# The experts gather x over its norm, and scale and shift go in as columns where the gathered rows leave PSUM

## The chip, the cores and the metric

The kernel runs on one core of one Trainium2 chip, in one launch. The metric is the time of the device for one execution, in microseconds (us): lower is better. A core has five engines with a queue of instructions each, which every engine works off in order: TensorE (PE; its weight loads are listed as PEld), VectorE (DVE), ScalarE (ACT), GpSimd (POOL) and SyncE (SP), which here issues the transfers from memory (DMA). Data are worked on in SBUF, which has 128 partitions; matmuls write into PSUM, which DVE and ACT read.

## The reference, cut to what matters

Two transformer blocks in a row on 256 tokens of width 1024, in float32. The first block has two layers, and each layer has a mixer (attention of several kinds) and a mixture of 16 experts. The change touches the mixture of experts alone:

```
sh_m, sc_m, g_m, shift_f, scale_f, gate_f = adaln(c, ada_w[layer], ada_b[layer])
h = rmsnorm(x, norm_ffn[layer]) * (1 + scale_f) + shift_f       # 256 x 1024
# grouped_moe(h, ...):
aff = sigmoid(h @ router_w)                  # 256 x 16 experts, in 4 groups of 4
# one group of experts is picked by aff + router_b, and 2 experts in it (TOP_K)
# each token's row h goes through its experts, weighted by aff over its sum:
#   y_e = (silu(h @ w_gate[e]) * (h @ w_up[e])) @ w_down[e]      # 1024 -> 512 -> 1024
x = x + gate_f * sum_e weight_e * y_e
```

rmsnorm divides each token's row by the root of its mean square (the factor is `rs` in the kernel) and multiplies by a gain per column. Scale, shift and gate depend on one condition vector `c`, so that they are the same for all tokens: one number for each of the 1024 columns. The kernel holds the scale with the gain in it as `mod[4]` and the shift as `mod[3]`, both 128x1024 with the same row in every partition.

## The kernel before

The first block's weights come through a ring of 12 slots of 1 MB each, which SP fills in the order of use: an expert's gate and up weights are two slots each, its down weights two. A slot is free again when the last matmul on it is done. The order of instructions on each engine is set when the program is built, by a scheduler that works with a time line of its own, and is then fixed; each engine's queue runs in that order and waits where an operand is not there.

The token rows are in `s.x[0]` and `s.x[1]`, 128 tokens each. `moe_body` first prepares the router:

- PE transposes x (L187, by way of `trans4`), ACT and DVE copy the transposes out (`hTf`). ACT and DVE sum the squares (L1913, L1914), POOL makes `rs` (L1916).
- The router's weights were multiplied by the scale ahead of time (`router_prep`, L1105 to L1120, which transposes `mod[4]` and `mod[3]` to have scale and shift along the partitions). So the logits are 8 matmuls with the transposed x (L1920), a copy `lg` (L1922), 4 small matmuls (L1925), then `z` with `rs` and the shift's part on DVE (L1927), and the sigmoid `aff` on ACT (L1928), which first loads its table.
- A chain of small DVE operations picks group and experts: `bz` (L1931), `s`, `gs`, `gm`, `gt`, `ge` (L1936 to L1950), `sel` (L1954, L1955), and its bf16 copy `selb` (L1957).
- PE counts the tokens of each expert with three small matmuls on `selb`, DVE makes each token's place `pos` (L1970) and from it the one-hot matrices `OH` (L1976): per expert 64 columns, one for each place.

Beside that chain the rows to be gathered are made: h = x * rs * mod[4] on DVE (L1984), + mod[3] on POOL (L1985), then the high part `hTh` on ACT (L1988) and the rest `hTl` on DVE (L1989). These two read h in steps of 8 elements (32 bytes), so that each block of 128 columns of the result is one k of 8, as the expert weights have it (column p * 8 + k in partition p).

`gather(b)` (L2011 to L2024) then forms the experts' inputs for four experts at a time: 32 matmuls, with 128 columns of `hTh` or `hTl` as weights and 256 columns of `OH` as the moving operand, into 4 banks of PSUM, which ACT copies to `xT`. It is called 4 times per layer. `gateup` (L2048) and `down` (L2066) are the experts' own matmuls, on two experts at a time. Tokens that find no place among the 64 of an expert go through an overflow loop (L2126 to L2232) that gathers them with the same operands (L2212, copy `xk` L2215); it runs once here, in the second layer.

While the router works, PE also has matmuls for the next scale, shift and gate rows (`ada`, L1046 to L1099): 8 matmuls of 512 columns for a row (L1095), `adat` on DVE (L1098), one matmul that spreads it over the partitions (L1057), and a copy `mod` (L1059, L1061).

The code around the change, with the profile's line numbers:

Of the kernel before, what the change touches and what calls it, by code (L numbers as in the profile page):

```python
# [57 lines left out]
class Kern:  # L58
# [125 lines left out]
    def trans4(s, src, n=4):  # L184
        p = s.bank("tp", (128, n, 128))
        for i in range(n):
            s.nc.tensor.transpose(p[:, i], src[:, i * 128:(i + 1) * 128], s.ident)  # L187
        return p

# [650 lines left out]
class Full(Kern):  # L840
# [108 lines left out]
    def setup1(s):  # L949
# [14 lines left out]
        nc.gpsimd.memset(s.rwg, 0.0)  # L964
        s.rlb = B1.tile([128, 16], F32, name="rlb")
        s.onesb = B1.tile([128, 128], BF, name="onesb")
        nc.gpsimd.memset(s.onesb, 1.0)
        s.trib = B1.tile([128, 128], BF, name="trib")
        s.rb = B1.tile([128, 16], F32, name="rb")
        s.late.append(lambda: nc.sync.dma_start(s.rwp, I["router_w"].rearrange("(k p) e -> p k e", p=128)))  # L970
        s.late.append(lambda: nc.sync.dma_start(s.rb, I["router_b"].partition_broadcast(128)))
# [133 lines left out]
    def router_prep(s):  # L1105

        nc, V = s.nc, s.nc.vector
        for j in range(2):
            p = s.trans4(s.mod[4][:, j * 512:(j + 1) * 512])
            V.tensor_tensor(s.rwg[:, 4 * j:4 * j + 4, 0:16], s.rwp[:, 4 * j:4 * j + 4], p[:, :, 0:16], op=OP.mult)  # L1110
            yield
        q = s.bank("bg", (128, 16))
        for j in range(2):
            p = s.trans4(s.mod[3][:, j * 512:(j + 1) * 512])
            sh = s.a2("sh")
            nc.scalar.copy(sh, p)
            for k in range(4):
                nc.tensor.matmul(q, sh[:, k], s.rwp[:, 4 * j + k], start=j + k == 0, stop=j + k == 4)
        V.tensor_copy(s.rlb, q)
        yield  # L1120
# [754 lines left out]
    def moe_srcs(s, l):  # L1875
# [4 lines left out]
        for e in range(0, 16, 2):  # L1880
            for w in (g, u):
                for h in range(2):
                    for i in range(2):
                        out.append((w[e + i].rearrange("(p k) n -> p k n", p=128)[:, 4 * h:4 * h + 4], True))
            for h in range(2):
                for i in range(2):
                    out.append((d[e + i].rearrange("(p k) n -> p k n", p=128)[:, 2 * h:2 * h + 2], True))
# [7 lines left out]
    def moe_body(s, l, end):  # L1895
# [10 lines left out]
        for t in range(2):  # L1906
            for j in range(2):
                p = s.trans4(s.x[t][:, j * 512:(j + 1) * 512])
                if t == 0:
                    nc.scalar.copy(hT[j][:, :, 0:128], p)  # L1910
                else:
                    V.tensor_copy(hT[j][:, :, 128:256], p)
# [8 lines left out]
        lg = s.a2("lg", (128, 256))  # L1921
        nc.scalar.copy(lg, p)  # L1922
        p = s.bank("bg", (128, 2, 16))
        for t in range(2):
# [31 lines left out]
        selb = A.tile([128, 2, 16], BF, name="selb")  # L1956
        V.tensor_copy(selb, sel)  # L1957
        W = f("W", 2, 16)
# [14 lines left out]
        def onehot(b):  # L1973
            for t in range(2):
                e = slice(4 * b, 4 * b + 4)
                V.tensor_tensor(OH[t][:, e], pos[:, t, e, None].to_broadcast([128, 4, 64]), s.C["io1"][:, None, :].to_broadcast([128, 4, 64]),  # L1976
                                op=OP.is_equal)

        hh = []
        for t in range(2):  # L1980
            h = hb[t]
            hi = s.hp.tile([128, D], F32R, name=f"hTh{t}")
            lo = s.hp.tile([128, D], F32R, name=f"hTl{t}")
            V.scalar_tensor_tensor(h, s.x[t], rs[:, t:t + 1], s.mod[4], op0=OP.mult, op1=OP.mult)  # L1984
            G.tensor_tensor(h, h, s.mod[3], op=OP.add)  # L1985

            hv, hiv, lov = h.rearrange("t (p k) -> t k p", k=8), *(x.rearrange("t (k p) -> t k p", k=8) for x in (hi, lo))
            nc.scalar.copy(hiv, hv)  # L1988
            V.tensor_tensor(lov, hv, hiv.bitcast(F32), op=OP.subtract)  # L1989
            hh.append((hi, lo))  # L1990
        OH += [s.sm.tile([128, 16, 64], F32R, name=f"OH{t}", tag="h", bufs=2) for t in range(2)]
# [19 lines left out]
        def gather(b):  # L2011
            for i in range(2):
                xT[2 * b + i] = A.tile([128, 8, 128], F32, name="xT", tag="xT", bufs=3)
            for c in range(0, 8, 2):
                p = s.bg()
                for cc in range(2):
                    first = True
                    for t in range(2):
                        for x in hh[t]:
                            nc.tensor.matmul(p[:, cc * 256:(cc + 1) * 256], x[:, (c + cc) * 128:(c + cc + 1) * 128], OH[t][:, 4 * b:4 * b + 4],  # L2020
                                             start=first, stop=t == 1 and x is hh[t][1])
                            first = False
                for i in range(2):
                    nc.scalar.copy(xT[2 * b + i][:, c:c + 2], p.rearrange("p (c i s) -> p c i s", c=2, i=2)[:, :, i])  # L2024

# [100 lines left out]
    def overflow(s, l, hh, pos, W, nx, cum):  # L2126
# [44 lines left out]
        with s.tc.For_i(0, n, 1):  # L2171
# [9 lines left out]
            for h in range(2):  # L2181
                for i, w in enumerate(("moe_w_gate", "moe_w_up")):
                    nc.sync.dma_start(*s.flat(wg[2 * h + i], I[w][l][e].rearrange("o (p k) n -> p (o k) n", p=128)[:, 4 * h:4 * h + 4]))
            tail()
# [23 lines left out]
            for c in range(8):  # L2208
                first = True
                for t in range(2):  # L2210
                    for x in hh[t]:
                        nc.tensor.matmul(p[:, c], x[:, c * 128:(c + 1) * 128], oh[:, t, 0], start=first, stop=t == 1 and x is hh[t][1])  # L2212
                        first = False
            xk = s.a2("xk", (128, 8, 64))
            nc.scalar.copy(xk, p)  # L2215
            p = s.bank("tp", (128, 2, 128))
# [49 lines left out]
```

## Time and profile before

| | before |
|---|---|
| median of 3 runs | 2464.49 us (2462.65 to 2467.65) |
| profiled execution | 2464.17 us |
| its span in the trace | 2462.4 us |
| mean granted TensorE clock | 0.972 of full speed |
| busy: PE, PEld | 2310.5 us (94%), 1636.8 us (66%) |
| busy: DVE, ACT, POOL | 1297.5 us, 1031.8 us, 411.6 us |

The span is the time from the first to the last event in the trace; 1.8 us of the execution lie around it. A busy share is an average over the program; what a change in one place is worth is read there. TensorE runs at one of two clocks, 1.2 and 2.4 GHz, and the trace tells what share of full speed was granted in a stretch.

### The profile page before, as it was taken

To read this page: it belongs to the slowest core of one execution; us is meant where nothing else is said; L and a number is where in the kernel's file an instruction comes from. 1 tells how busy PE (TensorE), PEld (TensorE's weight loads), DVE (VectorE), ACT (ScalarE), POOL (GpSimd) and SP (SyncE) were. 2 spreads that over 40 slices of the span, in tenths; PEclk is the share of its full clock that TensorE was granted. 3 is DMA by queue.
4 is the path that set the end of the run, shared out by engine and by line. 5 is a ranking of instruction groups with operands and counts; after the bars stand their busy time and mean duration, and the time that the engine had idled before them with its cause. 6 is when DMAs were issued, how large, how long until landed. Compare 5 with 4: busy or idle time off the path is not lost.

```text
span 2462.4 us, 32028 instructions
## 1 busy us (share of the span) xinstructions
PE 2310.5 (94%) x12635; PEld 1636.8 (66%) x12635; DVE 1297.5 (53%) x2047; ACT 1031.8 (42%) x1615; POOL 411.6 (17%) x356
## 2 busy tenths in 40 slices
PE   6999999989899898999888999999999997999999
PEld 4755433356443436888777788887887776788887
DVE  4455222255422226555777756555555877765554
ACT  3454111044211105445655564444444754564543
POOL 1001000010100002002468510000001439620000
PEclk8999999989999898999999999999999998999999
DMA  9677798966799795555333355654655442445552
GB/s 346 242 262 255 320 420 365 415 231 232 290 419 382 300 383 189 188 190 198 132 139 121 138 168 170 204 187 163 205 188 195 167 142 90 135 159 196 172 188 69
DMA packets 241657, 551.33 MB, mean 224 GB/s; under 512 B 12639, under 2 KB 113864, under 8 KB 216160
## 3 DMA queue, kind: packets, MB, share of 16 engines
q1 hardware_dynamic: 241504, 549.26, 61.9%
q8 instruction: 100, 1.64, 0.3%
q14 instruction: 53, 0.43, 0.1%
HBM read 548.15 MB, written 1.06 MB: 223 GB/s over the span
## 4 chain that ended last, share of the span: by engine, by line
PE 62%; DVE 8%; POOL 5%; issue 2%; ACT 2%; DVEq 0%; ACTq 0%; POOLq 0%
PE mm L135 10%; PE mm L137 10%; PE mm L136 10%; PE mm L2048 5%; PE m L135 4%; PE m L136 4%; PE m L137 4%; DVE lo L917 3%; PE m L2066 2%; PE tp L187 2%; PE bg L136 2%; PE bg L135 2%; PE bg L137 2%; POOL rb L597 1%; PE bg L2020 1%
## 5 line engine op out<-in xcount | busy, mean ns | idle before, releaser
L917 DVE TENSOR_TENSOR lo<-w,hi 128x1024 fp32r<-128x1024 f32 (+1 forms) x520 | 659.5, 1308 | 422.0 <-issue 117.7
L915 ACT CAST hi<-w 128x1024 fp32r<-128x1024 f32 (+1 forms) x524 | 519.6, 1040 | 464.5 <-DVE lo L917 352.6
L135 PE MATMUL mm<-hi,hTh 128*128 128x512 f32 (+2 forms) x1200 | 482.4, 404 | 16.4 <-DVE rx L594 8.7
L136 PE MATMUL mm<-lo,hTh 128*128 128x512 f32 (+2 forms) x1200 | 473.4, 395 | 1.0 <-DVE lo L917 1.0
L137 PE MATMUL mm<-hi,hTl 128*128 128x512 f32 (+2 forms) x1200 | 471.9, 394 | 2.1 <-DVE hTl L192 1.8
L135 PEld LDWEIGHTS mm<-hi,hTh 128*128 128x128 f32 x1200 | 228.9, 191 | 65.4 <-DVE rx L594 10.2
L137 PEld LDWEIGHTS mm<-hi,hTl 128*128 128x128 f32 x1200 | 228.8, 191 | 53.3 <-DVE hTl L192 4.2
L2048 PE MATMUL mm<-w,xT 128*64 128x512 f32 x1024 | 259.4, 600 | 2.9 <-DVEq L2171 1.6
L136 PEld LDWEIGHTS mm<-lo,hTh 128*128 128x128 f32 x1200 | 229.7, 192 | 45.1 <-DVE lo L917 1.8
L2048 PEld LDWEIGHTS mm<-w,xT 128*64 128x64 f32 x1024 | 80.8, 137 | 141.4 <-issue 136.5
L135 PE MATMUL m<-hi,hTh 128*128 128x512 f32 x384 | 156.0, 407 | 9.2 <-DVE rx L594 8.9
L137 PE MATMUL m<-hi,hTl 128*128 128x512 f32 x384 | 153.4, 399 | 0.6 <-DVE hTl L192 0.6
L136 PE MATMUL m<-lo,hTh 128*128 128x512 f32 x384 | 153.7, 400 | 0.0
L2066 PE MATMUL m<-w,hidT 128*64 128x512 f32 x512 | 123.7, 597 | 7.7 <-ACT hidT L2059 6.6
L2053 DVE TENSOR_TENSOR sl<-mm,sl 128x512 f32<-128x512 f32 x16 | 11.1, 691 | 160.9 <-PE mm L2048 116.4
L135 PEld LDWEIGHTS m<-hi,hTh 128*128 128x128 f32 x384 | 73.9, 193 | 26.8 <-DVE rx L594 10.2
L2066 PEld LDWEIGHTS m<-w,hidT 128*64 128x64 f32 x512 | 41.1, 136 | 72.8 <-issue 61.5
L2071 DVE SCALAR_TENSOR_TENSOR yf<-m,wsl,mod 128x512 f32<-128x512 f32 x32 | 24.0, 750 | 114.9 <-PE m L2066 113.2
L137 PEld LDWEIGHTS m<-hi,hTl 128*128 128x128 f32 x384 | 73.6, 192 | 16.2 <-DVE hTl L192 1.0
L136 PEld LDWEIGHTS m<-lo,hTh 128*128 128x128 f32 x384 | 73.9, 192 | 15.3 <-DVE lo L917 0.8
L204 POOL TENSOR_TENSOR rs<-ss,mhalf 128x1 f32<-128x1 f32 x18 | 11.0, 611 | 427.1 <-DVE ss L202 427.0
L191 ACT CAST hidh<-tp 128x256 fp32r<-128x256 f32 x88 | 32.3, 372 | 101.2 <-PE tp L187 101.1
(610 smaller groups left out, 3492.5 us busy)
## 6 DMA issues: line engine op xcount, KB each, us to landing
w<-in_ffn_w_in_dram SPq DMA_DIRECT2D x176, 512.0 KB, 4.9
w<-in_w_in_dram SPq DMA_DIRECT2D x84, 1024.0 KB, 4.9
w<-in_moe_w_gate_dram SPq DMA_DIRECT2D x64, 1024.0 KB, 10.8
w<-in_moe_w_up_dram SPq DMA_DIRECT2D x64, 1024.0 KB, 13.9
w<-in_moe_w_down_dram SPq DMA_DIRECT2D x64, 1024.0 KB, 12.3
w<-in_ada_w_dram SPq DMA_DIRECT2D x48, 1024.0 KB, 7.4
w<-in_ffn_w_out_dram SPq DMA_DIRECT2D x44, 1024.0 KB, 4.9
w<-in_ev_w_in_dram SPq DMA_DIRECT2D x10, 1024.0 KB, 6.6
```

Source lines behind the costliest of these rows:

```text
L135: nc.tensor.matmul(out, xh, wh, start=first, stop=False)
L136: nc.tensor.matmul(out, xh, wl, start=False, stop=False)
L137: nc.tensor.matmul(out, xl, wh, start=False, stop=last)
L187: s.nc.tensor.transpose(p[:, i], src[:, i * 128:(i + 1) * 128], s.ident)
L191: s.nc.scalar.copy(hi, p)
L597: G.tensor_tensor(b[:, :, o:o + 64], x[:, :, i:i + 64], sn[:, t, None, o:o + 64].to_broadcast([128, 4, 64]), op=OP.mult)
L915: a = s.nc.scalar.copy(hi[:, h], t[:, h]).ins
L917: b = eng.tensor_tensor(lo[:, h], t[:, h], hi[:, h].bitcast(F32), op=OP.subtract).ins
L2020: nc.tensor.matmul(p[:, cc * 256:(cc + 1) * 256], x[:, (c + cc) * 128:(c + cc + 1) * 128], OH[t][:, 4 * b:4 * b + 4], start=first, stop=t ...
L2048: nc.tensor.matmul(p[64 * i:64 * i + 64], xT[q][:, 4 * h + k, 64 * i:64 * i + 64], ws[i][:, k], start=h + k == 0, stop=h + k == 4)
L2066: nc.tensor.matmul(ps[n][64 * i:64 * i + 64], hT[:, 2 * h + k, 64 * i:64 * i + 64], ws[i][:, k, n * 512:(n + 1) * 512], start=h + k == 0, ...
L2071: V.scalar_tensor_tensor(yf, ps[n], wsl[:, q:q + 1], s.mod[5][:, n * 512:(n + 1) * 512], op0=OP.mult, op1=OP.mult)
```

## The change

What is gathered is no longer h, but x * rs, split in a high and a low part. Scale and shift, which stand along the partitions once the rows are gathered and transposed, are put in as one column each when a bank of gathered rows is read out of PSUM. The columns come from the transposes of `mod[4]` and `mod[3]` that `router_prep` makes anyway, into a new tile `mT` (128x16). The order of columns that the expert weights need now comes from the matmul's weight operand: the transposes and the gather read every 4th element of their rows (16 bytes apart), and the expert's gate and up weights and the router's weights are loaded in two halves of 512 rows, each with 4 rows per partition.

The evacuation of a gather's bank becomes two activations of 128x128 on ACT (scale and bias as columns) and two operations of 128x128 on DVE, instead of two copies of 128x256 on ACT. In the overflow loop `xk` is made by two operations on DVE instead of one copy on ACT.

```diff
+    def transp(s, src, j):
+        p = s.bank("tp", (128, 4, 128))
+        v = src[:, j * 512:(j + 1) * 512].rearrange("t (p k) -> t k p", k=4)
+        for k in range(4):
+            s.nc.tensor.transpose(p[:, k], v[:, k], s.ident)
+        return p
...
-            p = s.trans4(s.mod[4][:, j * 512:(j + 1) * 512])
+            p = s.transp(s.mod[4], j)
+            V.tensor_copy(s.mT[:, 4 * j:4 * j + 4], p[:, :, 0])
...
-            p = s.trans4(s.mod[3][:, j * 512:(j + 1) * 512])
+            p = s.transp(s.mod[3], j)
             sh = s.a2("sh")
             nc.scalar.copy(sh, p)
+            V.tensor_copy(s.mT[:, 8 + 4 * j:12 + 4 * j], sh[:, :, 0])
...
-                        out.append((w[e + i].rearrange("(p k) n -> p k n", p=128)[:, 4 * h:4 * h + 4], True))
+                        out.append((w[e + i, 512 * h:512 * h + 512].rearrange("(p k) n -> p k n", p=128), True))
...
-                p = s.trans4(s.x[t][:, j * 512:(j + 1) * 512])
+                p = s.transp(s.x[t], j)
...
         nc.scalar.copy(lg, p)
+        hh = []
+        for t in range(2):
+            hi = s.hp.tile([128, D], F32R, name=f"hTh{t}")
+            lo = s.hp.tile([128, D], F32R, name=f"hTl{t}")
+            nc.scalar.activation(hi, s.x[t], AF.Copy, scale=rs[:, t:t + 1])
+            hh.append((hi, lo))
+        lows = lambda t: V.scalar_tensor_tensor(hh[t][1], s.x[t], rs[:, t:t + 1], hh[t][0].bitcast(F32), op0=OP.mult, op1=OP.subtract)
+        lows(0)
...
-        V.tensor_copy(selb, sel)
+        q = V.tensor_copy(selb, sel).ins
+        s.after(lows(1).ins, q.name)
+        hh = [[x.rearrange("t (h p k) -> t h k p", h=2, k=4) for x in y] for y in hh]
...
-        hh = []
-        for t in range(2):
-            h = hb[t]
-            hi = s.hp.tile([128, D], F32R, name=f"hTh{t}")
-            lo = s.hp.tile([128, D], F32R, name=f"hTl{t}")
-            V.scalar_tensor_tensor(h, s.x[t], rs[:, t:t + 1], s.mod[4], op0=OP.mult, op1=OP.mult)
-            G.tensor_tensor(h, h, s.mod[3], op=OP.add)
-            hv, hiv, lov = h.rearrange("t (p k) -> t k p", k=8), *(x.rearrange("t (k p) -> t k p", k=8) for x in (hi, lo))
-            nc.scalar.copy(hiv, hv)
-            V.tensor_tensor(lov, hv, hiv.bitcast(F32), op=OP.subtract)
-            hh.append((hi, lo))
...
-                            nc.tensor.matmul(p[:, cc * 256:(cc + 1) * 256], x[:, (c + cc) * 128:(c + cc + 1) * 128], OH[t][:, 4 * b:4 * b + 4],
+                            nc.tensor.matmul(p[:, cc * 256:(cc + 1) * 256], x[:, (c + cc) // 4, (c + cc) % 4], OH[t][:, 4 * b:4 * b + 4],
...
-                for i in range(2):
-                    nc.scalar.copy(xT[2 * b + i][:, c:c + 2], p.rearrange("p (c i s) -> p c i s", c=2, i=2)[:, :, i])
+                for cc in range(2):
+                    m = s.mT[:, c + cc:c + cc + 1], s.mT[:, 8 + c + cc:9 + c + cc]
+                    for i in range(2):
+                        o, x = xT[2 * b + i][:, c + cc], p[:, cc * 256 + i * 128:cc * 256 + i * 128 + 128]
+                        if i:
+                            V.tensor_scalar(o, x, m[0], m[1], op0=OP.mult, op1=OP.add)
+                        else:
+                            nc.scalar.activation(o, x, AF.Identity, bias=m[1], scale=m[0])
...
-                        nc.tensor.matmul(p[:, c], x[:, c * 128:(c + 1) * 128], oh[:, t, 0], start=first, stop=t == 1 and x is hh[t][1])
+                        nc.tensor.matmul(p[:, c], x[:, c // 4, c % 4], oh[:, t, 0], start=first, stop=t == 1 and x is hh[t][1])
...
-            nc.scalar.copy(xk, p)
+            for i, o in enumerate((OP.mult, OP.add)):
+                V.tensor_tensor(xk, xk if i else p, s.mT[:, 8 * i:8 * i + 8, None].to_broadcast([128, 8, 64]), op=o)
```

Left out are the loads of the router's weights and of the overflow loop's expert weights, which are re-laid in the same way. `s.after` pins an instruction behind another in the scheduler's order.

The order of three places follows. A row gives the line in its own kernel, the operation, the tiles written and read, and the shape. First DVE in the second layer's router, from the choice of experts on; before, the two low parts `hTl` and the next row `adat` stand among the choosing operations:

```order
L1950 COPY_PREDICATED gt<-call,ge 128x128
L1940 TENSOR_REDUCE gm<-gs 128x2
L1989 TENSOR_TENSOR hTl_4607<-h,hTh_4606 128x1024
L1954 TENSOR_REDUCE sel<-gt 128x32
L1941 TENSOR_TENSOR gs<-gs,gm 128x8
L1942 TENSOR_TENSOR gs<-gs,call 128x8
L1098 SCALAR_TENSOR_TENSOR adat<-abias,ident,bg 128x512
L1943 TENSOR_REDUCE gm<-gs 128x2
L1989 TENSOR_TENSOR hTl_4613<-h,hTh_4612 128x1024
L1944 TENSOR_TENSOR gs<-gs,gm 128x8
L1955 SCALAR_TENSOR_TENSOR sel<-sel,gs 128x32
L1957 CAST selb<-sel 128x32
```

The same place on DVE in the changed kernel, whose lines from L188 on are numbered higher:

```order
L1961 TENSOR_REDUCE gm<-gs 128x2
L1975 TENSOR_REDUCE sel<-gt 128x32
L1962 TENSOR_TENSOR gs<-gs,gm 128x8
L1963 TENSOR_TENSOR gs<-gs,call 128x8
L1964 TENSOR_REDUCE gm<-gs 128x2
L1965 TENSOR_TENSOR gs<-gs,gm 128x8
L1976 SCALAR_TENSOR_TENSOR sel<-sel,gs 128x32
L1978 CAST selb<-sel 128x32
L1942 SCALAR_TENSOR_TENSOR hTl_4605<-x_71,rs_4559,hTh_4604 128x1024
L1982 TENSOR_TENSOR W<-aff,sel 128x32
L1107 SCALAR_TENSOR_TENSOR adat<-abias,ident,bg 128x512
L1993 SCALAR_TENSOR_TENSOR pos<-tp,sel 128x32
```

Nothing stands any more between the choice and `selb`; one low part and one `adat` stand between `selb` and `pos`. The other low part is further up, behind `z`.

Second, ACT in the second layer's router, before; `lg` is the copy of the logits, `aff` the sigmoid:

```order
L1922 COPY lg<-bg 128x256
L1928 ACT_TABLE_LOAD
L1928 ACTIVATE aff<-z 128x32
L1988 CAST hTh_4606<-h 128x1024
L1061 COPY mod_4622<-bg 128x512
L1988 CAST hTh_4612<-h 128x1024
```

And in the changed kernel:

```order
L1933 COPY lg<-bg 128x256
L1940 ACTIVATE hTh_4601<-x_70,rs_4559 128x1024
L1940 ACTIVATE hTh_4604<-x_71,rs_4559 128x1024
L1949 ACT_TABLE_LOAD
L1949 ACTIVATE aff<-z 128x32
```

Both high parts have moved ahead of the table load and the sigmoid.

Third, DVE in the second layer after the last of the eight one-hot matrices, in the changed kernel, where the first gather's banks are read out (`xT`); before, that work was ACT's alone:

```order
L1999 TENSOR_TENSOR OH_4652<-pos,call 128x256
L1999 TENSOR_TENSOR OH_4653<-pos,call 128x256
L2015 SCALAR_TENSOR_TENSOR nx<-tp,nx 128x16
L1986 TENSOR_TENSOR W<-W,den 128x32
L2038 TENSOR_SCALAR xT<-bg,mT 128x128
L2015 SCALAR_TENSOR_TENSOR nx<-tp,nx 128x16
L2038 TENSOR_SCALAR xT<-bg,mT 128x128
```

The first of DVE's reads of the banks stands behind all eight one-hot matrices, two of which the first gather needs.

## Rows read from the trace of the kernel before

**Rows 1.** Busy time by stretch: us, busy of each engine, PEclk, DMA share, GB/s

```profile
626.00:646.00 20.00, 11.59 (x81) 4.77 (x80) 17.93 (x38) 9.16 (x11) 6.37 (x3) 0.93 1.00 405
253.00:258.00 5.00, 4.84 (x28) 4.42 (x30) 3.24 (x15) 1.48 (x5) 0.00 (x0) 0.53 0.15 34
285.00:312.00 27.00, 27.00 (x138) 11.34 (x135) 6.83 (x11) 4.25 (x10) 0.00 (x0) 1.00 1.01 419
```

**Rows 2.** Chain of waits, 626 to 651 us: start, us, what

```profile
631.59 0.38 ACT lg L1922
...
635.30 1.17 DVE bz L1931
...
636.49 2.54 DVE s L1936 x4
...
639.83 1.91 DVE hTl L1989
...
642.20 0.66 DVE adat L1098
...
645.17 0.18 DVE selb L1957
...
646.48 1.19 PE bg L2020 x4
```

**Rows 3.** POOL's line L1985: duration in ns min/median/max, first and last start us, shapes

```profile
L1985 POOL TENSOR_TENSOR h<-h,mod x4: 2365/2852/3337, 238.3 to 636.4; 128x1024 f32<-128x1024 f32 x4
```

**Rows 4.** DVE's line L1936, in the same form

```profile
L1936 DVE TENSOR_TENSOR s<-bz x8: 160/168/2289, 244.0 to 638.9; 128x16 f32<-128x16 f32 x4, 128x8 f32<-128x8 f32 x4
```

**Rows 5.** Groups by form, ACT: count | busy us, mean ns | idle before, releaser

```profile
L915 ACT CAST hi<-w 128x1024 fp32r<-128x1024 f32 x512 | 511.4, 1047 | 460.0 <-DVE lo L917 351.2 <-issue 68.5 <-PE m L136 16.5
L2024 ACT COPY xT<-bg 128x256 f32<-128x256 f32 x64 | 20.9, 375 | 105.1 <-PE bg L2020 98.6 <-PE mm L2048 6.5
L2052 ACT ACTIVATE sl<-mm 128x512 f32<-128x512 f32 x16 | 9.6, 597 | 111.1 <-PE mm L2048 111.1
L1988 ACT CAST hTh<-h 128x1024 fp32r<-128x1024 f32 x4 | 8.4, 2090 | 3.6 <-POOL h L1985 3.6
L228 ACT ACTIVATE sgb<-m,rs 128x512 f32<-128x512 f32 x8 | 5.5, 688 | 3.6 <-PE bg L660 2.5 <-PE m L137 1.1
L1928 ACT ACT_TABLE_LOAD x2 | 2.6, 1283 | 0.0
L2215 ACT COPY xk<-bg 128x512 f32<-128x512 f32 x1 | 0.6, 586 | 7.2 <-PE bg L2212 7.2
```

**Rows 6.** Timeline of the second layer's sigmoid: start, us, what [idle before]

```profile
634.52 0.23 ACT L1928 ACTIVATE aff<-z 128x32 f32<-128x32 f32 x1 [1.26 <-DVE z L1927]
```

**Rows 7.** Groups by form, DVE, columns as for ACT

```profile
L917 DVE TENSOR_TENSOR lo<-w,hi 128x1024 fp32r<-128x1024 f32 x508 | 649.4, 1318 | 419.2 <-issue 117.7 <-PE mm L136 109.6 <-ACT sl L260 92.2
L1976 DVE TENSOR_TENSOR OH<-pos,call 128x256 fp32r<-128x256 f32 x16 | 5.7, 417 | 0.0
L1984 DVE SCALAR_TENSOR_TENSOR h<-x,rs,mod 128x1024 f32<-128x1024 f32 x4 | 5.0, 1281 | 1.7 <-POOL rs L1916 1.7
L1246 DVE COPY vsw<-mm 128x128 f32<-128x128 f32 x2 | 0.6, 280 | 0.0
```

**Rows 8.** Timeline of the first layer's router, PE

```profile
243.16 1.92 PE L1095 MATMUL bg<-w,cl 128*32 128x512 f32 x16
...
253.16 0.55 PE L2020 MATMUL bg<-OH,hTh 128*128 128x256 f32 x1 [0.80 <-DVE OH L1976]
```

**Rows 9.** Timeline of the first layer's router, DVE

```profile
247.92 0.74 DVE L1098 SCALAR_TENSOR_TENSOR adat<-abias,ident,bg 128x512 f32<-128x512 f32 x1
```

**Rows 10.** Timeline of the first layer's second gather, PE

```profile
275.21 0.28 PE L2020 MATMUL bg<-OH,hTl 128*128 128x256 f32 x1
...
276.17 0.28 PE L2020 MATMUL bg<-OH,hTl 128*128 128x256 f32 x1
```

**Rows 11.** Timeline, weight loads (PEld) of eight matmuls that move one column

```profile
18.29 0.97 PEld L1493 LDWEIGHTS tp<-ones,adat 128*128 128x128 f32 x8 [0.87 <-issue]
```

More of the change, by code (lines that the diff above doesn't have):

```diff
@@ L965, in setup1 @@
         s.rlb = B1.tile([128, 16], F32, name="rlb")
+        s.mT = B1.tile([128, 16], F32, name="mT")
         s.onesb = B1.tile([128, 128], BF, name="onesb")
@@ L969, in setup1 @@
         s.rb = B1.tile([128, 16], F32, name="rb")
-        s.late.append(lambda: nc.sync.dma_start(s.rwp, I["router_w"].rearrange("(k p) e -> p k e", p=128)))
+        s.late.append(lambda: nc.sync.dma_start(s.rwp.rearrange("p (h k) e -> p h k e", h=2), I["router_w"].rearrange("(h p k) e -> p h k e", p=128, k=4)))
         s.late.append(lambda: nc.sync.dma_start(s.rb, I["router_b"].partition_broadcast(128)))
@@ L2182, in overflow @@
                 for i, w in enumerate(("moe_w_gate", "moe_w_up")):
-                    nc.sync.dma_start(*s.flat(wg[2 * h + i], I[w][l][e].rearrange("o (p k) n -> p (o k) n", p=128)[:, 4 * h:4 * h + 4]))
+                    nc.sync.dma_start(*s.flat(wg[2 * h + i], I[w][l][e][:, 512 * h:512 * h + 512].rearrange("o (p k) n -> p (o k) n", p=128)))
             tail()
```

## The prediction

> **What bounds the kernel now.** I read the busy time by stretch first. In the experts' own stretch PE is busy for all of its 27.00 us and the transfers run at their full rate [rows 1]: whatever the change does there counts only if it makes PE slower. In the 20 us of the second layer's router it is DVE that is full, 17.93 of 20.00 us, and PE only 11.59 [rows 1]. So the router is where time can come out, and the gathers, which lie among the experts' matmuls, are where it can be lost.
>
> Next the chain of waits of that router [rows 2]. From the copy `lg` at 631.59 to the first gather's matmul at 646.48 it is a list of DVE operations. The reader is to see three things. The 16-way choices are tiny, yet four `s` take 2.54 us. Two `hTl` stand in the middle of the choice, 1.91 us each. And `adat` stands there too, for the next ada row.
>
> Why are the four `s` slow? Their line has a median of 168 ns and a maximum of 2289 [rows 4]. POOL's addition of the shift takes 2.4 to 3.3 us, twice per layer, the last from 636.4 on [rows 3], which is just when `bz` and `s` crawl [rows 2]. I take it that DVE is held up while POOL adds. The trace shows that they coincide, not that the one causes the other.
>
> **The change part by part.** In the second layer:
>
> 1. ACT now makes both high parts before it loads the sigmoid's table. Each is a pass over 1024 contiguous elements, 1.05 us by L915 [rows 5], with a column as scale, for which I add 0.1: L228 with such a column is at 0.688, L2215 without at 0.586 [rows 5]. `lg` ends at 631.97 [rows 2]; two such passes end at 634.27, the table (1.28) at 635.55, the sigmoid (0.23) at 635.8. Before it ended at 634.75 [rows 6], the table load lying in the 1.26 us in which ACT waited for `z`. So this costs 1.0 us at the start. DVE's first low part, 1.28 us like L1984 [rows 7], which has the same form, lies in that wait and costs nothing. Without that cover it would cost its 1.28.
>
> 2. Behind the sigmoid: `bz` 0.2 and four `s` at 0.17 by the median [rows 4], 0.9 in all instead of 635.30 to 639.03 [rows 2]; an `adat`, 0.7; the comparisons as before, 639.03 to 639.83, 0.8; and `sel` to `selb`, which before ran from 641.74 to 645.35 with an `adat` of 0.66 and an `hTl` of 1.91 in it, and so 1.0 without [rows 2]. That makes 3.4, so `selb` ends at 639.2 instead of 645.35.
>
> 3. Behind `selb` there now stand the second low part, 1.28, and the last `adat`, 0.66, ahead of `pos`. PE's three small count matmuls and everything behind `pos` wait for them: 641.2. From there to the first gather's matmul it took 646.48 - 645.35 = 1.1 before, of which I leave 0.9, as `W` is already counted beside the low part. The gather begins at 642.1 instead of 646.48: 4.4 us earlier.
>
> In the first layer the order is the same, but PE's second ada row sets the floor: its matmuls end at 243.16 + 1.92 = 245.08 [rows 8], and `adat` for it stands before `selb`. It ran at 247.92 before [rows 9], because DVE was busy with `hTl`. Now: 245.08 + 0.74 + `selb` 0.18 + low part 1.28 + one more 512-wide operation 0.7 + `pos` to gather 1.0 = 249.0, where the gather began at 253.16 [rows 8]. That is 4.2 us. The sigmoid's 1.0 us goes under, since PE's row ends later anyway.
>
> What is late next is then PE's ada rows in the first layer, and DVE's second low part with `adat` in the second.
>
> 4. The evacuation of the gathered rows. For each bank ACT has two activations of 128x128 in place of two copies of 128x256 at 0.375 [rows 5]; I put each at 0.27 (half the columns, but not half the time, as DVE's 128x128 at 0.28 shows [rows 7]) plus 0.2 for two columns as operands, 0.47. DVE has two of 128x128, 0.28 to 0.47 each. In the later gathers ACT and DVE have room: ACT is busy 4.25 of 27.00 us and DVE 6.83 [rows 1]. So they cost nothing there. In the first gather DVE's part stands behind eight one-hot matrices at 0.42 or less [rows 7], two of which the gather itself needs, while PE, at a granted clock of 0.53 [rows 1], needs some 1.7 us for a bank. I put 0.5 us per layer, between nothing and 1.5 (four one-hots that PE does not wait for at present): 1.0.
>
> 5. The overflow loop runs once. `xk` took 0.586 on ACT [rows 5]; it is now two operations of 128x512 on DVE, each about half of L917's 1.318 [rows 7], 0.69 with its start. PE waits for it directly: 2 x 0.69 - 0.59 = +0.8.
>
> 6. Copies of columns into `mT`, four per layer, some 0.2 us each, lie on DVE while the layer's mixer still runs on PE: nothing; if they were uncovered, 1.6 in all. The re-laid loads have the same bytes in the same 8 KB per partition, and they are not what PE waits for in the experts' stretch, which PE fills [rows 1]: nothing. POOL's additions and DVE's two products h go; their gain is in steps 2 and 3.
>
> 7. The weight operand read at every 4th element, in 256 gather matmuls (64 of them in first gathers), 32 transposes of x and 32 of `mod`. No row shows this. From below: nothing, since ACT reads PSUM at the same 16-byte step in L2052 at 0.597, beside 0.586 for a plain copy of that size [rows 5]. From above: ACT's pass over SBUF at a 32-byte step, 2.09 against 1.05 by L1988 and L915 [rows 5], which is 1.0 ns more for an element, 0.13 us more for 128 columns. There is no cover for it: the later gathers run at 275.21 to 276.17, eight steps, 0.12 each [rows 10], and weight loads by themselves, with one column moved, take 0.97 for eight, 0.12 each [rows 11]. The load is as long as the matmul. A gain I exclude, as nothing is read less. I take nothing, since L2052 has the very step of the change, and keep 0.13 for the range.
>
> Of step 7 the Trainium skill has a rule in SBUF — State Buffer, section "Door 1: The DMA port swizzle (why `[64,N]` ≈ `[32,N]`)": SBUF lines are 16 bytes, full rate needs at least two accesses to the same line, and four fp32 is given as how far one can stride for free. By its figure for the stride, step 7 is nothing and the sum is the one below; by its two accesses per line, a step of 16 bytes touches a new line each time and pays, which is the first rival. L1988's doubling at 32 bytes agrees with both halves and decides between neither.
>
> Sum: -4.4 - 4.2 + 1.0 + 0.8 = -6.8 us. The earlier gather carries through to the end, since PE works without a break behind it [rows 1]. From the profiled span, 2462.4 - 6.8 = 2455.6, and with the 1.8 us around it 2457.4. That execution, 2464.17, is 0.3 under the median of the runs. I say **2457**.
>
> **The rivals.** *First, the strided weight load is slower (slower than before).* The place is PE in gathers 2 to 4, 96 matmuls per layer, and the transposes, 64 in all. If the load doubles from 0.11 to 0.22, 192 x 0.10 + 64 x 0.10 = 26 us are added: 2457 + 26 = 2483. By L1988's price of 0.13 it is 33: 2490. In the first gather and the overflow, at half clock, the matmul is long enough to cover some of it. It decides from 6.8 / 256 = 0.027 us per load on. For it speaks that the load has no cover [rows 10, 11] and that a 32-byte step does double ACT's pass; against it, that the 16-byte step costs ACT nothing in PSUM.
>
> *Second, the time is given back at once (no change).* PE's ada matmuls and the spreading of `adat` sit between the router and the gather, in a stretch where the clock falls to 0.53 [rows 1]; they may now end last, and the first gather's banks may wait for DVE behind all its one-hots: 1.5 us per layer instead of 0.5, and 1.0 more per layer for the ada rows. That takes 4 of the 6.8: 2461. For it: in the first layer PE's row at 245.08 already sets the floor. Against it: in the second the ada matmuls are not on the chain behind `bz`.
>
> *Third, DVE is not slow because of POOL (the change does not do what it says).* Then `bz` and `s` stay at 3.7 us, 2.8 more in the second layer, while in the first PE's row still hides most of it: 2460.
>
> **How the numbers follow.** Forecast 0.57, with a range of its own of 2451 to 2460, the lower end if the first gathers also run at full clock (32 matmuls at 5.00 / 28 = 0.18 against 0.12 [rows 1, 10], 2 us per layer). First rival 0.23, of which I give half to prices below a full doubling. Second 0.13, third 0.07. Within 0.2% (4.9 us, about what can be told here from no change) fall the second, most of the third and a little of the forecast: 0.19. Faster 0.58, slower 0.23. The range reaches from 2449 to the full doubling, 2483; above it I leave 0.1, below 0.05.
>
> **What would show it.** Right: gather matmuls at 0.12 in the later gathers and transposes at an unchanged pace; `bz` to `s` under 1 us; no `hTl` between the choice and `selb`; the first gather some 4 us sooner behind the mixer's last matmul in both layers, and equal times from there to the end of the layer. Wrong: a gather pace of 0.15 or more, which turns the sign; the first gather's banks waiting for DVE's `xT`; or PE idle before the gather for `adat` instead of `OH`.

## The result and the profile after

The changed kernel takes 2483.87 us (median of 4 runs, 2482.29 to 2486.17), the kernel before 2464.83 (4 runs): a ratio of 1.0077, 95% interval 1.006 to 1.0095. It is slower by 19 us, where 2457 was forecast. It is what the first rival gave for a doubled weight load, 2483, and 0.9 us above the range. Two executions further down, one of x7_pairs (3682.93 us) and one of the kernel before (3548.29 us), had a mean granted clock of 0.58 and 0.65 and are left out of all ranges and ratios.

First the busy time by stretch in the changed kernel: the two routers up to the first gather, and the experts' 27 us of [rows 1]. The columns are those of [rows 1].

```profile
232.00:247.40 15.40, 9.16 (x70) 3.62 (x70) 11.93 (x38) 5.57 (x9) 0.71 (x1) 1.00 0.89 346
638.40:655.10 16.70, 12.22 (x82) 5.28 (x80) 11.50 (x36) 6.68 (x10) 0.69 (x1) 0.90 0.99 389
285.00:312.00 27.00, 27.00 (x124) 11.78 (x123) 6.39 (x12) 3.94 (x8) 0.00 (x0) 1.00 1.01 418
```

The routers are shorter and DVE has room in them. In the experts' stretch PE is busy for 27.00 us as before, but gets 124 matmuls done in it instead of 138.

The chain of waits of the second layer's router in the changed kernel (start, us, what) answers to [rows 2]:

```profile
643.92 0.14 ACT lg L1933
...
644.19 2.19 ACT hTh L1940 x2
...
646.40 1.28 ACT L1949
...
647.70 0.24 ACT aff L1949
...
647.96 0.19 DVE bz L1952
...
650.84 2.69 PE bg L1104 x16
...
653.56 0.75 DVE adat L1107
654.30 0.11 DVE pos L1993
...
655.54 0.35 PE bg L2030 x2
```

`bz` is at 0.19 instead of 1.17, and the four `s` and both `hTl` have left the chain. The first gather's matmul starts at 655.05 (the chain has it from 655.54, where the matmul ahead of it ends), so that from the end of `lg` to the gather it is 11.0 us instead of 14.5. New behind `bz` is PE's ada row, `bg` L1104, which before stood ahead of it.

Then the gather itself. The timeline of PE in the changed kernel, the first layer's second gather, answers to [rows 10]:

```profile
270.04 0.40 PE L2030 MATMUL bg<-OH,hTl 128*128 128x256 f32 x1
270.27 0.40 PE L2030 MATMUL bg<-OH,hTh 128*128 128x256 f32 x1
270.51 0.40 PE L2030 MATMUL bg<-OH,hTl 128*128 128x256 f32 x1
270.74 0.40 PE L2030 MATMUL bg<-OH,hTh 128*128 128x256 f32 x1
```

The pace, from one matmul's start to the next one's, is 0.233 us instead of 0.12, at full clock. The groups of weight loads by form (busy us, mean ns), of the kernel before:

```profile
L2020 PEld LDWEIGHTS bg<-OH,hTl 128*128 128x128 f32 x128 | 26.5, 207 | 6.5 <-issue 6.5
...
L187 PEld LDWEIGHTS tp<-ident,x 128*128 128x128 f32 x32 | 3.5, 140 | 1.4 <-ACT hTf L1910 1.0
```

and of the changed kernel:

```profile
L2030 PEld LDWEIGHTS bg<-OH,hTl 128*128 128x128 f32 x128 | 42.1, 329 | 6.5 <-issue 6.5
...
L195 PEld LDWEIGHTS tp<-ident,x 128*128 128x128 f32 x32 | 4.3, 208 | 0.9 <-ACT hTf L1921 0.8
```

Every load from a row read at each 4th element has become longer, in the gather from 0.207 to 0.329 (as listed, with the tail that overlaps the next one). In the transposes the loads are shorter to begin with: at the step they are listed at 0.208, like the gather's before, and their median pace goes from 0.109 to 0.121 only.

At half clock the step costs little in the one place that shows it by itself. The gather of the overflow loop ran at a granted clock of 0.50 in both kernels, with matmuls that move 64 columns only. Its loads and matmuls (duration in ns min/median/max), before and after:

```profile
L2212 PEld LDWEIGHTS bg<-ohk,hTh x16: 288/333/333, 810.9 to 817.2; 128*128 128x128 f32 x16
L2212 PE MATMUL bg<-ohk,hTh x16: 401/401/423, 810.9 to 817.3; 128*128 128x64 f32 x16
...
L2228 PEld LDWEIGHTS bg<-ohk,hTh x16: 308/330/330, 827.6 to 834.5; 128*128 128x128 f32 x16
L2228 PE MATMUL bg<-ohk,hTh x16: 419/419/441, 827.6 to 834.6; 128*128 128x64 f32 x16
```

A load takes 0.333 us there without the step and 0.330 with it, and the pace goes from 0.213 to 0.233.

The spans add up so. The first layer's first gather starts 5.8 us earlier, the second's, counted from the end of the first layer's experts, 3.8 us. From first gather to the end of the experts it takes 18.2 and 10.5 us more. If PE's time is put down to each line from one matmul's start to the next one's, the gathers alone take 14.4 and 12.7 us more, 27.1 of these 28.7. After the experts of the second layer the two kernels differ by 0.3 us.

### The profile page after: what moved, and what is told of

Read it like the earlier page. It is cut to its first block, busy times and chain, and to the rows that moved or that the text cites. A ratio compares the mean times of both kernels' runs of the same rounds, so it can differ in the third digit from the quotient of the medians.

```text
span 2481.8 us, 32106 instructions
## 1 busy us (share of the span) xinstructions
PE 2336.5 (94%) x12635; PEld 1662.3 (67%) x12635; DVE 1311.1 (53%) x2117; ACT 1034.7 (42%) x1614; POOL 399.9 (16%) x352
## 4 chain that ended last, share of the span: by engine, by line
PE 62%; DVE 8%; POOL 5%; ACT 2%; issue 1%; DVEq 0%; POOLq 0%; ACTq 0%
PE mm L135 10%; PE mm L137 9%; PE mm L136 9%; PE mm L2064 5%; PE m L135 4%; PE m L136 4%; PE m L137 4%; DVE lo L925 3%; PE m L2082 2%; PE tp L187 2%; PE bg L135 2%; PE bg L136 2%; PE bg L137 2%; PE bg L2030 1%; POOL rb L605 1%
## 5 line engine op out<-in xcount | busy, mean ns | idle before, releaser
L135 PEld LDWEIGHTS mm<-hi,hTh 128*128 128x128 f32 x1200 | 228.9, 191 | 65.4 <-DVE rx L602 10.1
L135 PEld LDWEIGHTS m<-hi,hTh 128*128 128x128 f32 x384 | 73.9, 193 | 26.7 <-DVE rx L602 10.1
L2040 ACT ACTIVATE xT<-bg,mT 128x128 f32<-128x128 f32 x64 | 28.6, 457 | 142.7 <-PE bg L2030 131.3
L2038 DVE TENSOR_SCALAR xT<-bg,mT 128x128 f32<-128x128 f32 x64 | 25.6, 408 | 99.1 <-ACT xT L2040 99.0
L2104 DVE TENSOR_TENSOR x<-bg,x 128x512 f32<-128x512 f32 x64 | 41.6, 686 | 66.0 <-PE bg L2102 66.0
## 6 DMA issues: line engine op xcount, KB each, us to landing
w<-in_moe_w_up_dram SPq DMA_DIRECT2D x64, 1024.0 KB, 10.3
```

The costliest lines, as they stand in the source:

```text
L135: nc.tensor.matmul(out, xh, wh, start=first, stop=False)
L2038: V.tensor_scalar(o, x, m[0], m[1], op0=OP.mult, op1=OP.add)
L2040: nc.scalar.activation(o, x, AF.Identity, bias=m[1], scale=m[0])
L2104: V.tensor_tensor(xs, p, xs, op=OP.add)
```

## The experiments

Two theories stood against each other. 'Load': weights read at a 16-byte step load at 0.23 us and PE has nothing to cover that. 'Evacuation': PE is held because DVE and ACT now share the reading of each bank. This table sums up all kernels; the stages are read from PE's timeline in one profiled execution each (first gather's start in the first layer; from there to the end of its experts; from there to the second layer's first gather; from there to the end of its experts), the pace is the median from one gather matmul to the next. The diffs are cut to the expressions that change.

| kernel | median us | ratio, 95% | 1st gather | experts 1 | between | experts 2 | pace |
|---|---|---|---|---|---|---|---|
| before | 2464.83 | | 253.2 | 248.0 | 145.3 | 278.8 | 0.12 |
| changed | 2483.87 | 1.006 to 1.0095 | 247.4 | 266.2 | 141.5 | 289.3 | 0.234 |
| x1_before_step | 2464.01 | 0.9983 to 1.0002 | 254.7 | 262.0 | 146.4 | 266.1 | 0.235 |
| x1b_before_step | 2483.79 | 1.0062 to 1.0094 | 248.7 | 264.0 | 143.9 | 286.6 | 0.234 |
| x2_read_step | 2460.31 | 0.9973 to 0.9991 | 249.5 | 246.1 | 143.9 | 280.7 | 0.12 |
| x3_no_step | 2459.20 | 0.9962 to 0.9995 | 253.3 | 255.8 | 141.5 | 276.3 | 0.12 |
| x4_steps | 2470.70 (1 run) | | 248.0 | 259.7 | 141.3 | 282.2 | by step |
| x5_pool | 2493.52 (1 run) | | 252.9 | 267.3 | 144.8 | 289.4 | 0.234 |
| x6_write_step | 2462.61 | 0.9978 to 0.9996 | 250.4 | 244.7 | 144.4 | 284.7 | 0.12 |
| x7_pairs | 2459.40 | 0.9964 to 0.9985 | 248.6 | 247.1 | 142.1 | 282.6 | 0.12 |
| x8_late_high | 2457.25 | 0.9961 to 0.9984 | 248.7 | 250.6 | 141.9 | 279.2 | 0.12 |
| x9_before_pairs | 2456.43 | 0.9967 to 0.9996 | 250.4 | 248.9 | 143.8 | 273.0 | 0.12 |

The first gathers of a layer are slower than the pace in the table where half clock was granted: 0.213 before. The experiments' ratios are against runs of the kernel before on the same chip, with medians of 2464.95 (x1 to x4), 2465.09 (x1b to x7) and 2463.86 (x8, x9).

**The step alone, in the kernel before, first try** (x1_before_step).

```diff
-  x[:, (c + cc) * 128:(c + cc + 1) * 128]
+  x.rearrange("t (h p k) -> t h k p", h=2, k=4)[:, (c + cc) // 4, (c + cc) % 4]
```

> The kernel before, in which the gather alone reads its weight operand at every 4th element (16 bytes apart); its columns come out in another order than the reference's, so only the time counts. Theory 'load': a load at this step takes 0.23 us instead of 0.12, whatever else is in the kernel. Then the gathers' pace is 0.23, and 192 matmuls x 0.114 + 64 x 0.02 for the first gathers at half clock = +23 us: about 2488. Rival 'evacuation': PE is slowed in the changed kernel because DVE and ACT share the reading of the banks; then nothing changes here: 2464, pace 0.12.

The pace became 0.235 and the first layer's experts took 14.0 us more, and yet the median was 2464.01. That is a miss of the experiment, not of the theory: as columns came out in another order, the second layer's router saw other data, no expert overflowed, and the trace holds no matmul of L2212, so that the second layer lost the overflow loop and became shorter. The pace can be used, the total can't.

**The same with the data of before** (x1b_before_step). The high and low parts are written in the order that makes the step right:

```diff
-  hv, hiv, lov = h.rearrange("t (p k) -> t k p", k=8), ...("t (k p) -> t k p", k=8) for hi, lo
+  hv, hiv, lov = h.rearrange("t (p h k) -> t h p k", h=2, k=4), ...("t (h p k) -> t h p k", h=2, k=4) for hi, lo
```

> The kernel before, in which the gather's and the overflow's weight operands are read at every 4th element, with the high and low parts written in the order that makes this right (so that all the data, and the overflow with them, are those of the kernel before). For that ACT and DVE read h in runs of 4 neighbours, 32 bytes apart. Theory 'load': gather pace 0.23; 13 us more per layer from the first gather to the layer's end, 1.4 in the overflow; less up to 1 us per pass if runs of 4 are read at full rate (ACT 1.05 us instead of 2.09, by theory 'line'): 2464.9 + 26 - 4 = 2487. Rival 'evacuation' (the changed kernel loses by the split reading of the banks): 2461 to 2465.

It is as slow as the changed kernel, 2483.79, with nothing of the change in it but the step in the gather and the overflow. 'Evacuation' falls. That the two totals agree to 0.1 us is chance: its experts' stretches are 23.8 us longer than before where the changed kernel's are 28.7, and its first gathers come 5.9 us sooner instead of 9.6. Its timeline of PE:

```profile
272.95 0.39 PE L2021 MATMUL bg<-OH,hTh 128*128 128x256 f32 x1
273.18 0.39 PE L2021 MATMUL bg<-OH,hTl 128*128 128x256 f32 x1
273.42 0.39 PE L2021 MATMUL bg<-OH,hTh 128*128 128x256 f32 x1
```

There is more to read in it. ACT now reads runs of four neighbours 32 bytes apart, and its pass has gone from 2.09 [rows 5] to the time of a contiguous one (groups by form, mean ns):

```profile
L1988 ACT CAST hTh<-h 128x1024 fp32r<-128x1024 f32 x4 | 4.2, 1045 | 5.5 <-POOL h L1985 5.5
```

and the first gathers begin 4.5 and 1.4 us sooner.

**The step taken out of the gather** (x2_read_step). ACT and DVE read x at the step when they make the parts; the gather is contiguous, all else as changed.

```diff
+  s.x[t][:, c].rearrange("t (p k) -> t k p", k=4)     # read by ACT and DVE, halves of 512
-  x[:, (c + cc) // 4, (c + cc) % 4]
+  x[:, (c + cc) * 128:(c + cc + 1) * 128]
```

> The changed kernel, in which ACT and DVE read x at every 4th element when they make the high and low parts, so that the gather's and the overflow's weight operands are contiguous; the evacuation stays split. Theory 'load': gather pace 0.12, the 28.7 us that were lost behind the first gather's start come back, and the first gathers are faster than before if they run at full clock (64 x 0.09 = 6). The router keeps most of its 9.6 us: ACT's and DVE's reads at 16 bytes may cost up to 1 us each pass, 2 us per layer. About 2465 - 9.6 - 4 + 3 = 2454. Rival 'evacuation': pace stays at 0.23 and the time near 2484.

The experts' stretches are back at 246.1 and 280.7, 526.8 in all as before. Of the router's 9.6 us only 5.1 are left, since ACT and DVE now pay for the step (groups by form, mean ns):

```profile
L1953 ACT ACTIVATE hTh<-x,rs 128x512 fp32r<-128x512 f32 x8 | 9.2, 1236 | 0.0
...
L1945 DVE SCALAR_TENSOR_TENSOR hTl<-x,rs,hTh 128x512 fp32r<-128x512 f32 x8 | 8.9, 1138 | 0.3
```

Two halves of ACT make 2.47 us, where one contiguous pass of 1024 took 1.14 in the changed kernel.

**Writing at a step** (x6_write_step): as x2, with the pieces turned around, `"t (p k) -> t p k"` for the source and `"t (k p) -> t p k"` for the parts, so that x is read in order and the parts are written element by element 128 elements (512 bytes) apart, not at the 4 that the expectation names.

> The changed kernel, in which ACT and DVE read x in order and write the high and low parts at a step of 4 elements, so that the gather's weight operands are contiguous (DVE reads the high part at that step too). If only reading at 16 bytes is slow, ACT's halves of 128x512 take 0.7 us instead of 1.24, and the time is below the variant that reads at the step (2460.3): about 2455. If writing is as slow as reading, 2460.

On ACT, this writing takes 1198 ns for a half, about what reading at 16 bytes does. DVE, which here also reads the high part 512 bytes apart, takes 1141, no more than in x2. Writing at 16 bytes itself was not run.

```profile
L1953 ACT ACTIVATE hTh<-x,rs 128x512 fp32r<-128x512 f32 x8 | 8.3, 1198 | 0.0
```

**No step anywhere** (x3_no_step). The weights come with row k * 128 + p in partition p.

```diff
-  w[e + i, 512 * h:512 * h + 512].rearrange("(p k) n -> p k n", p=128)
+  w[e + i].rearrange("(k p) n -> p k n", p=128)[:, 4 * h:4 * h + 4]
```

> The changed kernel without any step: weights loaded with row k * 128 + p in partition p (2 KB pieces instead of 8 KB), transposes and gathers contiguous. Theory 'load': gather pace 0.12 and the whole router gain: about 2465 - 9.6 - 5 = 2450. Rival 'pieces': four times as many pieces lower the transfer rate in the experts' stretch from 419 GB/s; at a tenth less, some 24 us of waiting per layer, so 2490 and more.

The pace is 0.12, and the transfers do slow down, but less than feared: 394 and 399 GB/s in 300 to 400 us, where the kernel before has 419 and 420 (busy time by stretch):

```profile
300.00:350.00 50.00, 48.59 (x239) 21.54 (x237) 16.27 (x31) 9.06 (x19) 0.00 (x0) 1.00 1.04 394
350.00:400.00 50.00, 45.69 (x196) 15.97 (x196) 9.59 (x15) 3.88 (x7) 0.18 (x2) 1.00 1.03 399
```

The kernel was to take 2450 and took 2459.20. In the profiled execution its first gather begins as late as before, at 253.3: the granted clock was 0.73 in 232 to 247 us, where the changed kernel had 1.00. Its runs scatter from 2456.20 to 2468.84, and the profiled one is among the longer. Whether the slower transfers make that scatter was not settled.

**Which step costs** (x4_steps). Each of a layer's four gathers has a step of its own. The columns come out in another order here too, so that only the pace can be used.

```diff
+  k = (1, 2, 4, 8)[b]
+  x.rearrange("t (h p k) -> t h k p", p=128, k=k)[:, c // k, c % k]
```

> The changed kernel, in which the four gathers of a layer read their weight operands at different steps: 4, 8, 16 and 32 bytes (columns in another order than the reference's; the overflow contiguous; only the pace counts). Theory 'line': a load is slow when each element lies in a line of 16 bytes of its own: 0.12, 0.12, 0.23, 0.23. Rival 'contiguity': anything but neighbours is slow: 0.12, 0.23, 0.23, 0.23. Rival 'distance': the price grows with the step: 0.12, 0.15 to 0.18, 0.23, 0.4 or more.

PE's timeline, two rows from each of the first layer's gathers, at 4, 8, 16 and 32 bytes:

```profile
249.13 0.28 PE L2033 MATMUL bg<-OH,hTh 128*128 128x256 f32 x1
249.25 0.28 PE L2033 MATMUL bg<-OH,hTl 128*128 128x256 f32 x1
...
295.72 0.28 PE L2033 MATMUL bg<-OH,hTh 128*128 128x256 f32 x1
295.84 0.28 PE L2033 MATMUL bg<-OH,hTl 128*128 128x256 f32 x1
...
325.77 0.40 PE L2033 MATMUL bg<-OH,hTh 128*128 128x256 f32 x1
326.00 0.40 PE L2033 MATMUL bg<-OH,hTl 128*128 128x256 f32 x1
...
413.72 0.41 PE L2033 MATMUL bg<-OH,hTl 128*128 128x256 f32 x1
413.97 0.40 PE L2033 MATMUL bg<-OH,hTh 128*128 128x256 f32 x1
```

By the medians of these four gathers: 0.120, 0.120, 0.234, 0.244. At full clock two elements in each 16 bytes are free for the loads, one is not, and a step of 32 bytes adds next to nothing. 'Line' holds; 'contiguity' and 'distance' fall.

**POOL back** (x5_pool). Two additions that nothing reads:

```diff
+  G.tensor_tensor(hb[t], hh[t][0].bitcast(F32), s.mod[3], op=OP.add)
```

> The changed kernel with two additions of 128x1024 on POOL, whose results nothing reads, at the place where the kernel before has them (they start when a high part is done). Theory 'POOL holds DVE up': bz and the four s take 2 to 3.7 us again instead of 0.6, and the gathers begin 2 to 3 us later. Rival 'coincidence': bz and s stay at 0.6 us.

The first gathers begin 5.5 and 3.3 us later than in the changed kernel. Not the `s` suffer here but what lies beside the additions: the first low part at 3.49 instead of 1.28, and `bz` at 2.32 instead of 0.19. DVE's timeline:

```profile
237.26 3.49 DVE L1942 SCALAR_TENSOR_TENSOR hTl<-x,rs,hTh 128x1024 fp32r<-128x1024 f32 x1
240.68 2.32 DVE L1954 TENSOR_TENSOR bz<-aff,rb 128x32 f32<-128x32 f32 x1
242.92 0.73 DVE L1107 SCALAR_TENSOR_TENSOR adat<-abias,ident,bg 128x512 f32<-128x512 f32 x1
```

and POOL's:

```profile
237.31 5.64 POOL L1945 TENSOR_TENSOR h<-hTh,mod 128x1024 f32<-128x1024 f32 x2 [1.33 <-ACT hTh L1940]
```

`bz` ends within 0.1 us of the second addition. It goes both ways: that addition, which began 1.1 us before the low part ended, took 3.32 us, the first one 2.37. `adat`, which reads one operand from PSUM, tells nothing here, as POOL is done by then; but in the kernel before one `adat` ran from 634.55 on, inside POOL's addition from 633.08 to 636.41, and took its usual 0.75. That POOL holds DVE up, which the prediction took from a coincidence, is shown. The Trainium skill has it in SBUF — State Buffer, "Who interferes with whom": a DVE instruction with two inputs from SBUF contends with a GpSimd one that reads SBUF, and the loser waits for the whole instruction. The 2.32 us of `bz` agree.

**Pairs** (x7_pairs). If two elements in a line are free, the parts can be stored so that the gather steps by 8 bytes and ACT and DVE read x in pairs, 16 bytes apart.

```diff
+  o = [y[:, 512 * u:512 * u + 512].rearrange("t (p k) -> t p k", k=2) for y in hh[t]]
+  s.x[t].rearrange("t (p u k) -> t u p k", u=2, k=2)[:, u], o[0], o[1]
...
+  x[:, (c + cc) // 4, (c + cc) % 4 // 2, c % 2 + cc]     # in "t (u h p k) -> t h u k p"
```

> The changed kernel with the high and low parts stored so that the gather reads every 2nd element (8 bytes apart), and ACT and DVE read x in pairs of neighbours, 16 bytes apart. By theory 'line' both are free, as each line of 16 bytes is used twice: gather pace 0.12, ACT's passes of 512 at 0.7 us, the router's gain of 9.6 us whole, the first gathers up to 4 us faster: 2464.9 - 9.6 - 3 = 2452. By the rival 'contiguity' (only neighbours are read at full rate) ACT's passes take 1.2 us and the time is that of the variant that reads at a step, 2460.

The pace is 0.12, ACT's half is at 0.780 (0.7 was expected; in x2 1.236), and the kernel is faster than the one before, 0.9964 to 0.9985. Its gain is 5.7 us, not 13: the gathers begin 4.6 and 3.2 us sooner, but the second layer's experts take 3.8 us more. By PE's time from start to start that is in the experts' down matmuls, 62.5 us against 58.6; why, is left open.

ACT's group by form, then two rows of PE's timeline:

```profile
L1952 ACT ACTIVATE hTh<-x,rs 128x512 fp32r<-128x512 f32 x8 | 5.6, 780 | 0.0
```

```profile
270.43 0.28 PE L2042 MATMUL bg<-OH,hTl 128*128 128x256 f32 x1
270.56 0.28 PE L2042 MATMUL bg<-OH,hTh 128*128 128x256 f32 x1
```

**High parts behind the sigmoid** (x8_late_high).

```diff
-  nc.scalar.activation(hiv, xv, AF.Copy, scale=rs[:, t:t + 1])
+  s.after(nc.scalar.activation(hiv, xv, AF.Copy, scale=rs[:, t:t + 1]).ins, sg.name)     # sg: the sigmoid
```

> The kernel of pairs (8-byte step in the gather), in which ACT makes the high parts behind the sigmoid instead of ahead of it, and DVE both low parts behind selb. If the high parts are on the path, as the chain of the changed kernel shows them (2.2 us), the sigmoid comes 3.1 us earlier (four passes of 0.78), and 1.5 us of low part are added behind selb: some 1.5 us per layer, 2459.4 - 3 = 2456. If PE's ada rows set the first gather's start instead, nothing: 2459.

2457.25, some 2 us under x7, but the runs overlap (2455.51 to 2458.97 here, 2455.78 to 2461.20 there). The gathers begin no sooner, so the reason that I gave is not confirmed.

**The kernel before, with pairs alone** (x9_before_pairs).

```diff
+  hv, hiv, lov = h.rearrange("t (p u k) -> t u p k", u=4, k=2), ...("t (u p k) -> t u p k", u=4, k=2) for hi, lo
+  x.rearrange("t (u p k) -> t u k p", u=4, k=2)[:, (c + cc) // 2, (c + cc) % 2]     # gather and overflow
```

> The kernel before (scale and shift put in by DVE and POOL ahead of the gather, banks copied out by ACT alone), in which only the order of the high and low parts is changed: h is read in pairs of neighbours, 32 bytes apart, and the gather reads its weights at every 2nd element. It tells how much of the gain at the router is due to reading at full rate alone. Theory 'reading': ACT's pass 1.1 to 1.2 us instead of 2.09, gathers 3 to 5 us earlier over both layers, pace 0.12: 2465 - 4 = 2461. Theory 'POOL': as POOL still adds, and holds DVE up, little is gained: 2464 or more.

It has the lowest median, 2456.43, with POOL and all else as before. Five of 7 runs lie from 2453.78 to 2459.75, two at 2465.6, so that its ratio, 0.9967 to 0.9996, is not told apart from that of x7 and x8. ACT's pass took 1.139 instead of 2.09. Neither theory gave the total (2461, or 2464 and more): of the 10.3 us by which the profiled execution is shorter than that of the kernel before, 4.3 are gathers that begin sooner and 5.8 lie in the second layer's experts, which neither speaks of. Why is left open. What the runs do tell is that moving scale and shift behind the gather, with POOL's additions gone, brings nothing measurable over the pairs alone. The chain of x9 still shows POOL's hold on DVE:

```profile
633.13 1.17 DVE bz L1931
...
634.32 2.55 DVE s L1936 x4
```

## Why the prediction was wrong, point by point

- Step 7 failed: "I take nothing, since L2052 has the very step of the change". L2052 reads PSUM, the gather's weights lie in SBUF, and the one is no row for the other. The nearest row in SBUF was L1988, at twice the step and with one element in each 16 bytes like it; x4 shows that at full clock these two cost a load nearly the same, 0.244 and 0.234. Its bound, 0.13 us per load, was close to the measured 0.114. The first rival was the case. That its 2483 fits to 0.9 us is in part luck: it put 19.2 us on the later gathers and 6.4 on the transposes and nothing on the first gathers; the later gathers took 22.8 more, the first ones 4.3 and the transposes 0.8 (64 x 0.012), and it went with 8.6 us of gain at the routers, which gave 9.6.
- Of the Trainium skill's rule in SBUF — State Buffer, "Door 1: The DMA port swizzle (why `[64,N]` ≈ `[32,N]`)", the half that asks for two accesses to a line of 16 bytes agrees with what was measured here, the loads at full clock: 8 bytes 0.120, 16 bytes 0.234, 32 bytes 0.244, and ACT's pass of 1024 at 1.05 in runs of four, 2.47 at single elements in two halves. The half by which four fp32 can be stepped for free does not agree with 0.234; the measurement decides. The two halves answer differently at this step; the prediction left them undecided and let a row of another memory decide.
- That "there is no cover" was right for the later gathers. The transposes were priced too high: their loads were 0.140 as listed, not 0.207, and their pace rose by 0.012 each instead of 0.10. The rival expected less loss at half clock because a longer matmul would cover some of the load. In the overflow the loss is small, 0.020 per load, but not by cover: its matmuls move 64 columns, and its loads take 0.333 us without the step and 0.330 with it.
- Steps 1 to 3 held, and but for one wait their sizes too. In the second layer, from the end of `lg`, the sigmoid was to end after 3.8 us and did after 3.9; `selb` after 7.2 and did after 7.25. Then `adat` waited 0.95 us for PE's ada row, which step 3 had not as the last to come, but the second rival had, at 1.0: the gather began after 11.0 instead of 10.1. The first layer gained 5.8 instead of 4.2: the granted clock was 1.00 there in 232 to 247 us, 0.89 before, and PE's second ada row ended 1.2 us sooner, at 243.84 instead of 245.08.
- The third rival (DVE is not slow because of POOL) is out, by x5.
- Step 4 and 5: ACT's 128x128 with two columns takes 457 ns, DVE's 408, as put (0.47; 0.28 to 0.47). `xk` takes 0.692 + 0.691 instead of 0.586, the 0.8 us of step 5. The 0.5 us per layer that step 4 put on DVE's part of the first gather did not come: PE waited for no bank there. It waited for DVE's `xT` once, 0.5 us at 745.8 in the second layer's third gather; before, it waited so long for ACT's copies in each layer's third gather.
- The first rival should have had more than the forecast: nothing stood behind "nothing" but a row of another memory, while the row of the same memory spoke against it, and there was no cover.

## What to carry to other kernels

Where a step moves from an engine off the path to TensorE's weights, look first at whether the load has any cover: here eight loads alone took as long as eight matmuls, so each nanosecond of a load was a nanosecond of PE. Price a step by a row of the same memory with the same number of elements in 16 bytes, not by one of the same distance in another memory. And if an order of columns is needed, spread it over two passes so that each takes two neighbours at a time: here the gather kept its pace of 0.12, and ACT's half took 0.780 us instead of 1.236.

## What was not expected of the hardware

A step of 16 bytes in SBUF about doubles the time per element of ACT (1.236 us for 512 against 1.145 for 1024), of DVE (1.138 for 512 against 1.28 for 1024) and, at full clock, of TensorE's weight load (0.234 against 0.120, by the gathers' pace); writing single elements 512 bytes apart takes ACT as long (1.198). By the pace of matmuls that wait for their loads, the strided load takes the same 0.233 us at half clock (the overflow) and at full clock (the gathers), while the contiguous one goes from 0.213 to 0.120.
